# A paced weight stream under a scan, and an MLP whose weights are scaled a piece ahead, in a hybrid transformer block

## The chip, the cores and the metric

The kernel runs on one core of a Trainium2 chip. The metric is the time of one execution on the device in microseconds (us). Engines: PE (TensorE, matrix products), DVE (VectorE), ACT (ScalarE), POOL (GpSimd) and SP (issues transfers). TensorE's clock has two levels, 1.2 and 2.4 GHz; the profile gives the granted clock of a stretch as a share of the upper one.

## The reference, cut to what matters

```python
zl = modulate(rms_norm(xl, norm1_g), ml[0], ml[1]) @ w_in       # 2048 latent tokens, and 256 context tokens
yl_gla  = gla_mixer(...)     # gated linear attention, both directions
yl_rwkv = rwkv7_mixer(...)   # delta-rule state, both directions, 6 heads
yl_ret  = retention(...)     # 4 heads, both directions, then silu(g) * rms-normed output
xl = xl + ml[2] * (concat([yl_gla, yl_rwkv, yl_ret]) @ w_out)
hl = modulate(rms_norm(xl, norm2_g), ml[3], ml[4])
xl = xl + ml[5] * (square(relu(hl @ mlp_w1)) @ mlp_w2)          # 1024 -> 4096 -> 1024
return rms_norm(xl, final_norm_g)
```

Everything is float32; the width is 1024, chunks have 64 tokens.

## The kernel before

Tensors of weights and activations are split into a high and a low half (f16 pairs, or two fp32r parts), and a product is three matmuls. The work comes in stages, one after the other: the part of the input projection that the RWKV scan needs (to about 590 us), the scan stage (to about 2095 us), the output projection (to about 2320 us), the first half of the MLP (tokens 0 to 1023, to about 3085 us) and its second half.

**The scan stage** is written by a planner, `Order`. Its streams are generators; each writes some instructions and yields the planner time until it may go on, or a condition. `pick` takes, of the streams whose condition holds and which are ready, the one with the least position `pos()`; a stream's position runs evenly from `first` to `last` over its yields. All matmuls of the stage are recorded with one line, L1065; one goes by tiles. The streams are:

- the RWKV scan: `prepare` for each direction makes a block's factors, and the chains (`rw_chains`, L945) run 108 steps of 64 tokens one after the other, forward and backward together. A step has three products in PSUM (`ptf`, `ptb`): the state's, copied by ACT to `Ts`; the corrections', negated into `UV` half by DVE (L964) and half by ACT (L965); and the new state's, which DVE adds to the old into `SUV` (L975). `rw_finish` normalizes finished blocks of tokens.
- `ip_stream` (L450): the rest of the input projection, 86 tiles of 128 tokens in five groups of columns (`STREAM_T`), each 24 matmuls with tile `rh`, in pieces of six; its results go to memory (`zt`), where the mixers read them. In this text it is "the stream". `k.streamed` counts its finished groups. Its PSUM pool has one bank.
- the mixers: GLA heads, then the two retention pairs (`ret_pair`, L1655), which start when their group is finished; what `follow` adds (the row-wise finish, transposes `fpt`) runs beside them.

**The MLP** goes over 16 pieces fp of the hidden width, 256 columns each. `mlp_w1` (L1857) loads a piece's weights, takes the greatest magnitude (DVE reductions L1867, then `over_partitions`: a PE transpose L1850, a reduction L1852, a PE product with ones L1853), makes the scale, and from sums of the weight's blocks seven f16 weights `wo` (L1842, L1879, L1880). `hidden` makes seven products (L2041, bank `pu`) and from them the squared hidden values as `uh` and `ul` (L2068, L2070). Then eight blocks of 128 tokens t each take twelve products with w2 (L2105), added to `acc` by DVE (L2107): sixteen additions a piece. The second half reads the weights that the first has written (`w1d`, `w2d`).

The first piece's weight is made in `out_proj`, and the last norm there (`norms(7)`) and w2 come ahead of the first hidden products.

Code beside these stages is ordered by the tile framework's scheduler.

Of the kernel before, what the change touches and what calls it, by code (L numbers as in the profile page):

```python
# [22 lines left out]
P = 128  # L23
# [420 lines left out]
STREAM_T = [TV, TG[0:3], RET_T[0], RET_T[1], TG[3:5]]  # L444


def ip_stream(k, wp, ps):
# [10 lines left out]
    for g, cols in enumerate(STREAM_T):  # L458
# [485 lines left out]
def rw_chains(k, gs, nxt, j, blk, yT, done, bp, ps):  # L944
# [6 lines left out]
    for c in range(4):  # L951
        pt = [ps.tile([P, 3, 64], F32, tag="pc" + x, name="pt" + x, bufs=1) for x in "fb"]
# [87 lines left out]

class Order:

# [5 lines left out]
    def add(self, gen, first, last, count, lead=1e9):  # L1048
        s = Stream(gen, first, last, count, lead)
        s.ready = self.t  # L1050
        self.streams.append(s)
        return s
# [28 lines left out]
    def run(self):  # L1081
# [572 lines left out]
def ret_pair(k, p2, pool, ps):  # L1654
# [6 lines left out]
    nc.sync.dma_start(V.rearrange("p c h n -> p c (h n)"), grp(0, T, vc))  # L1661
# [4 lines left out]
    def keys(t0, n):  # L1666
        c0, nch = t0 // P, n // P
        if t0:
# [13 lines left out]
    yield 4  # L1682
    kd = keys(*TOKB[0])
    yield 4
    for bi, (t0, n) in enumerate(TOKB):
# [15 lines left out]
        if bi + 1 < len(TOKB):  # L1701
            kd = keys(*TOKB[bi + 1])
# [70 lines left out]
    k.fin = follow(k, 5, finish_rows(k, pool, ps, Y, ms, 2, 64, gc, k.col("rng", p2), 768 + 128 * p2))  # L1773


def follow(k, n, gen):
# [6 lines left out]
    return k.order.add(steps(), k.mix.pos() - 20, k.mix.pos() + 5, 10)  # L1783


def mixers(k, ps):
# [3 lines left out]
    with tc.tile_pool(name="mix", bufs=1) as mp:  # L1790
# [55 lines left out]
def over_partitions(k, ps, pool, x):  # L1846

    nc = k.nc
    pt = ps.tile([P, 512], F32, tag="p1", name="pmx")
    nc.tensor.transpose(pt[0:1, 0:P], x, k.ident)  # L1850
    m = pool.tile([1, 1], F32, tag="mx1", name="mx1")
    nc.vector.tensor_reduce(m, pt[0:1, 0:P], axis=AX.X, op=ALU.max)  # L1852
    nc.tensor.matmul(pt[:, P : P + 1], k.ones[0:1], m, start=True, stop=True)  # L1853
    return pt[:, P : P + 1]


def mlp_w1(k, fp, sp, tag, bufs, ws, wp, eng):  # L1857

# [404 lines left out]
```

## Time and profile before

| what | value |
|---|---|
| median of 3 runs | 3725.27 us (3703.3, 3725.27, 3731.29) |
| profiled execution | 3744.08 us, its span 3742.3 us |
| mean granted TensorE clock | 0.908 |
| PE busy | 3411.3 us, 91% |
| DVE, ACT, POOL busy | 2437.2, 1394.9, 685.7 us |

The views are read from the profiled execution, which took 0.5% longer than the median.

### The profile page before, as it was taken

The numbers are of one execution on the slowest core, as the hardware profiler recorded it, in microseconds if no ns is written. First come the engines' busy times: TensorE is split into PE (matmuls) and PEld (weight loads), VectorE is DVE, ScalarE is ACT, GpSimd is POOL, SyncE is SP. The second block draws the span as 40 slices with busy tenths as digits, with TensorE's granted clock in tenths as the row PEclk, the third lists the DMA queues.
The fourth block names the chain that finished last, engine by engine and source line by source line (L and its number), as shares of the span: only waits on it lengthen the run. The fifth ranks groups of instructions, "written<-read, shape, count | busy, mean of one in ns | idle before, by whom it ended". The sixth has DMA issues, their size and how long they took to land. (4 is left out here: it accounts for less than half of the span.)

```text
span 3742.3 us, 62893 instructions
## 1 busy us (share of the span) xinstructions
PE 3411.3 (91%) x23616; PEld 2272.0 (61%) x23616; DVE 2437.2 (65%) x5128; ACT 1394.9 (37%) x3097; POOL 685.7 (18%) x863
## 2 busy tenths in 40 slices
PE   6798999999998999989998598899999999999997
PEld 2444446676666766767776486555555556666665
DVE  7458785668856576674665488876777665444446
ACT  3355553344436255252434234333333342112113
POOL 3224443234413222222332100000000010000001
PEclk7898998988978799778888799999999999999998
DMA  7988876446634436333332387633333365223222
GB/s 228 202 229 252 249 214 198 133 135 191 163 115 126 104 105 153 76 102 104 96 98 84 136 201 258 218 130 123 125 124 124 111 184 186 89 89 119 89 89 97
DMA packets 534217, 547.09 MB, mean 146 GB/s; under 512 B 276475, under 2 KB 407366, under 8 KB 533134
## 3 DMA queue, kind: packets, MB, share of 16 engines
q1 hardware_dynamic: 533904, 542.99, 48.7%
q8 instruction: 188, 3.08, 0.4%
q14 instruction: 125, 1.02, 0.1%
HBM read 331.18 MB, written 187.55 MB: 139 GB/s over the span
## 5 line engine op out<-in xcount | busy, mean ns | idle before, releaser
L2041 PE MATMUL pu<-H,wo 128*128 128x512 f16 x2688 | 623.9, 386 | 23.9 <-ACT wo L1879 20.8
L2107 DVE TENSOR_TENSOR acc<-acc,pz 128x512 f32<-128x512 f32 x512 | 348.0, 686 | 376.2 <-PE pz L2105 372.8
L2041 PEld LDWEIGHTS <-wo 128*128 128x128 f16 x2688 | 254.2, 99 | 357.1 <-issue 58.4
L2105 PE MATMUL pz<-w2h,uh 128*128 128x512 f32 x1024 | 441.2, 431 | 26.0 <-ACT uh L2068 23.9
L2105 PE MATMUL pz<-w2l,uh 128*128 128x512 f32 x1024 | 411.4, 402 | 0.0
L2105 PE MATMUL pz<-w2h,ul 128*128 128x512 f32 x1024 | 396.8, 396 | 0.0
L1065 PE MATMUL pz<-rwh,rh 128*128 128x384 f16 (+1 forms) x1376 | 289.3, 342 | 8.5 <-DMA rh<-hd 5.9
L2120 POOL TENSOR_TENSOR acc<-acc,fg 128x1024 f32<-128x1024 f32 x10 | 24.0, 2416 | 1457.6 <-ACT acc L2119 1457.6
L1065 PEld LDWEIGHTS <-rh 128*128 128x128 f16 x2064 | 198.0, 105 | 134.6 <-issue 37.5
L2105 PEld LDWEIGHTS pz<-w2h,uh 128*128 128x128 f32 x1024 | 199.9, 195 | 83.6 <-ACT uh L2068 26.1
L2105 PEld LDWEIGHTS pz<-w2l,uh 128*128 128x128 f32 x1024 | 199.9, 195 | 41.4
L2105 PEld LDWEIGHTS pz<-w2h,ul 128*128 128x128 f32 x1024 | 195.8, 191 | 43.3
L2065 ACT ACTIVATE u<-u 128x512 f32<-128x512 f32 x64 | 36.8, 622 | 476.5 <-DVE s L2059 476.5
L425 PEld LDWEIGHTS <-wh 128*128 128x128 f16 (+2 forms) x1072 | 111.0, 107 | 151.1 <-issue 44.6
L425 PE MATMUL pz<-hT_hi,wh 128*128 128x512 f16 (+5 forms) x536 | 127.2, 379 | 42.0 <-ACT zs L428 23.8
L2053 ACT ACTIVATE s<-pu,iv 128x512 f32<-128x512 f32 x96 | 65.5, 686 | 259.3 <-PE pu L2041 258.0
L1065 PE MATMUL pz<-rwl,rh 128*128 128x384 f16 (+1 forms) x688 | 143.7, 339 | 0.0
L1065 PE MATMUL pg<-Z,BK 64*128 64x128 f32 (+1 forms) x864 | 138.4, 339 | 4.0 <-issue 1.9
L1988 PE MATMUL pz<-woh,yh 128*128 128x512 f32 x256 | 100.2, 406 | 28.2 <-DMA x<-in_w_out_dram 21.6
L1065 PEld LDWEIGHTS pg<-Z,BK 64*128 64x128 f32 x864 | 115.8, 233 | 16.8 <-issue 5.8
L425 PE MATMUL pz<-hT_hi,wl 128*128 128x512 f16 (+5 forms) x536 | 122.8, 366 | 0.0
L425 PE MATMUL pz<-hT_lo,wh 128*128 128x512 f16 (+5 forms) x536 | 121.0, 363 | 0.0
(526 smaller groups left out, 6915.8 us busy)
## 6 DMA issues: line engine op xcount, KB each, us to landing
rh<-hd SPq DMA_DIRECT2D x86, 512.0 KB
st<-in_mlp_w_dram SPq DMA_DIRECT2D x64, 512.0 KB
w1d<-wo SPq DMA_DIRECT2D x112, 256.0 KB
wo<-w1d SPq DMA_DIRECT2D x112, 256.0 KB
x<-in_x_dram SPq DMA_DIRECT2D x32, 512.0 KB
mw<-in_mod_w_dram SPq DMA_DIRECT2D x32, 512.0 KB
w2d<-w2h SPq DMA_DIRECT2D x32, 512.0 KB
w2d<-w2l SPq DMA_DIRECT2D x32, 512.0 KB
```

What stands on the lines that cost most here:

```text
L425: nc.tensor.matmul(pz[:M, o : o + step], a[:, kk, 0:M], b[:, kk, t0 + o : t0 + o + step], start=(i == 0), stop=(i == 23))
L1065: return op(out, lhs, rhs, **kw)
L1988: nc.tensor.matmul(pz, a[:, kk], w[:, kk, 512 * hf : 512 * hf + 512], start=(kk + i == 0), stop=(kk == KD - 1 and i == 2))
L2041: nc.tensor.matmul(bank, W[o][:, a, kk], H[o][:, 4 * b + kk], start=(i == 0), stop=(i == 11))
L2053: nc.scalar.activation(s, product(o), AF.Copy, scale=iv)
L2065: nc.scalar.activation(r, r, AF.Relu)
L2105: nc.tensor.matmul(pz, U[q][tb][u][:, ts], W2[q][w][:, cs], start=(i == 0), stop=(i == 5))
L2107: nc.vector.tensor_add(a[:, cs], a[:, cs], pz)
L2120: nc.gpsimd.tensor_mul(a, a, fg)
```

## The change

In the scan stage: `ip_stream` is paced. It gets a `period` in planner time, `PACE` (3.3) times the width of its piece over 384; `pick` takes it as soon as it is due and leaves it out before, except where nothing else is ready. Its PSUM pool has two banks. The last retention gates' group goes ahead of the second retention pair's columns. The chains' two directions share one PSUM tile, `pt`. `ret_pair` waits for tiles of the stream (`k.tile`) in place of whole groups and loads V block by block; the finish of pair 0 waits for four groups in place of five, and its position is later.

In the MLP: `mlp_w1` is split. `mlp_w1_load` loads the weight, sums its squares by ACT (L1880), and gets the scale from the sum's inverse root (`norm_scale`: one product with ones, L338, and five small DVE operations); it runs one piece earlier. `mlp_w1` is a generator that makes one of the seven weights behind each token block of the piece before. `over_partitions` is gone. `hidden` is the function `mlp_hidden`, and the first piece's call stands in `out_proj`, ahead of w2 and `norms(7)`.

```diff
-STREAM_T = [TV, TG[0:3], RET_T[0], RET_T[1], TG[3:5]]
+STREAM_T = [TV, TG[0:3], RET_T[0], TG[3:5], RET_T[1]]
...
+            k.stream.period = PACE * n / 384
...
+            k.tile = ti + 1
             yield 0
-        k.streamed += 1
+        k.streamed, k.tile = k.streamed + 1, 0
...
-        pt = [ps.tile([P, 3, 64], F32, tag="pc" + x, name="pt" + x, bufs=1) for x in "fb"]
+        pc = ps.tile([P, 2, 3, 64], F32, tag="pc", name="pt", bufs=1)
+        pt = [pc[:, d] for d in range(2)]
...
+        paced = [s for s in open_ if s.period and s.ready <= self.t]
+        for s in paced:
+            if s.due <= self.t or len(open_) == 1:
+                return s
+        if len(open_) > 1:
+            open_ = [s for s in open_ if not s.period] or open_
         head = min(s.pos() for s in open_)
         near = [s for s in open_ if s.pos() <= head + s.lead] or open_
         ready = [s for s in near if s.ready <= self.t]
         if ready:
             return min(ready, key=Stream.pos)
+        for s in paced:
+            if s.due <= self.t + 3 * s.period:
+                return s
...
+            if s.period:
+                s.due = max(s.due, self.t - s.period) + s.period
...
+    def there(i):
+        t0, n = TOKB[i]
+        return lambda: (k.streamed, k.tile) >= (2 + 2 * p2, (t0 + n) // P)
+
-    yield 4
+    yield there(0)
     kd = keys(*TOKB[0])
...
         if bi + 1 < len(TOKB):
+            yield there(bi + 1)
             kd = keys(*TOKB[bi + 1])
...
-    k.fin = follow(k, 5, finish_rows(k, pool, ps, Y, ms, 2, 64, gc, k.col("rng", p2), 768 + 128 * p2))
+    k.fin = follow(k, 4 + p2, finish_rows(k, pool, ps, Y, ms, 2, 64, gc, k.col("rng", p2), 768 + 128 * p2))
...
-    return k.order.add(steps(), k.mix.pos() - 20, k.mix.pos() + 5, 10)
+    return k.order.add(steps(), k.mix.pos() - 10, k.mix.pos() + 15, 10)
...
-                yield lambda: k.streamed >= 3 + p2
                 yield from ret_pair(k, p2, pool, ps)
...
-        nc.vector.tensor_reduce(am[:, h : h + 1], st[h], axis=AX.XY, op=ALU.max, apply_absolute_value=True)
-    nc.vector.tensor_max(am[:, :1], am[:, :1], am[:, 1:])
-    ar = sp.tile([P, 1], F32, tag="ar", name="ar")
-    nc.vector.tensor_scalar(ar, over_partitions(k, k.p1, sp, am[:, :1]), 1e-30, 2.0 ** -14, ALU.max, ALU.mult)
-    s = sp.tile([P, 1], F32, tag="s", name="s")
-    iv = k.iv[:, fp : fp + 1]
-    nc.vector.reciprocal(s, ar)
-    nc.vector.tensor_mul(iv, ar, k.h_inv2)
-    W = {}
+        sq = jp.tile([P, D], BF16, tag="sq", name="sq", bufs=1)
+        nc.scalar.activation(sq.rearrange("p (k n) -> p k n", k=4), st[h], AF.Square, accum_out=am[:, h : h + 1])
+    nc.vector.tensor_add(am[:, :1], am[:, :1], am[:, 1:])
+    s, ar = norm_scale(k, k.p1.tile([P, 512], F32, tag="p1", name="pnrm")[:, 0:1], k.w1s, am[:, :1])
+    nc.vector.tensor_mul(k.iv[:, fp : fp + 1], ar, k.h_inv2)
+    return st, s
...
+        yield o, w
...
+        U0 = mlp_hidden(k, H, up, W0, k.iv[:, 0:1])
         k.g2 = mod_row(k, w2, 3)
+        W2 = [mlp_w2(k, q, w2) for q in range(2)]
         norms(7, xs, ss[:, 14:16])
-        W2 = [mlp_w2(k, q, w2) for q in range(2)]
...
+        loaded = None if half else mlp_w1_load(k, 1, wp, "st", 2, wp)
...
-                W1 = mlp_w1(k, fp, (wp, wp0)[fp % 2], "st", 2, 1, k.w1, nc.vector)
                 W2 = [mlp_w2(k, 2 * fp + q, w2p) for q in range(2)]
-            U = hidden(*W1)
+            U = mlp_hidden(k, H, up, W1, k.iv[:, fp : fp + 1]) if fp or half else U0
+            following = iter(()) if half or fp == NF - 1 else mlp_w1(k, fp + 1, *loaded, (wp, wp0)[(fp + 1) % 2], 1, k.w1, nc.vector)
+            if not half and fp < NF - 2:
+                loaded = mlp_w1_load(k, fp + 2, (wp0, wp)[fp % 2], "st", 2, wp)
+            W1 = {}
...
+                W1.update([x for x in (next(following, None),) if x])
...
-            fps = es.enter_context(tc.tile_pool(name="iprps", bufs=1, space=PSUM, side="right"))
+            fps = es.enter_context(tc.tile_pool(name="iprps", bufs=2, space=PSUM, side="right"))
...
-            k.order.add(ip_stream(k, fp, fps), 0, 312, 345, 4)
+            k.stream = k.order.add(ip_stream(k, fp, fps), 0, 312, 345, period=PACE)
```

How the instructions stand then is read from the order of each engine's instructions. First PE at the stream's last product (`pz<-rwh,rh`) in the scan stage, before: `pm`, `pn`, `pk` are of `rw_finish`, `fpt` of the retention finish, `rpt` of the last retention pair.

```order
L1065 MATMUL pz<-rwh,rh 128x256
L1065 MATMUL py<-GB,UVb 64x64
L1065 MATMUL pm<-yT,bones 128x256
L1065 MATMUL pgt<-fsg,wg_1455 128x256
L1065 MATMUL pm<-yT,bones 128x256
L1065 MATMUL pgt<-fsg,wg_1455 128x256
L1065 MATMUL pn<-bones,sqf 128x2 x4
L1065 MATMUL pk<-ident,sqf 128x128 x2
L1065 MATMUL fpt<-ident,rY 128x128 x4
L1065 MATMUL rpt<-ident,rK 128x128 x4
L1065 MATMUL pk<-ident,sqf 128x128 x2
```

The same place, the stream's last product, after the change (`pt` is the chains' shared tile, `pg` a factor's product in `prepare`, `fpt<-ident,gY` the finish of a GLA head):

```order
L1073 MATMUL pz<-rwh,rh 128x384
L1073 MATMUL pt<-UVf,BKT 64x64 x2
L1073 MATMUL pt<-UVb,BKT 64x64 x2
L1073 MATMUL fpt<-ident,gY 96x128 x4
L1073 MATMUL py<-Z,SUVf 64x64 x2
L1073 MATMUL py<-Z,SUVb 64x64
L1073 MATMUL pk<-ident,sqf 128x128 x2
L1073 MATMUL pt<-SUVf,Z 64x64 x2
L1073 MATMUL pt<-SUVb,Z 64x64 x2
L1073 MATMUL py<-Z,SUVb 64x64
L1073 MATMUL pg<-Z,BK 128x128 x4
L1073 MATMUL pt<-Tsf,XT 64x64 x2
```

Before, the stream's last product stands behind the chains' last, among finish and retention; now chains, factors and finishes follow it.

PE in the first half of the MLP, around the product with ones that makes a scale, before (rows `pz` are the first products with w2 of the same piece):

```order
L2041 LDWEIGHTS wo
L2041 MATMUL pu<-H,wo 128x512
L1850 MATMUL pmx<-ident,am 1x128
L1853 MATMUL pmx<-mx_33529,ones 128x1
L2105 MATMUL pz<-w2h,uh 128x512
L2105 MATMUL pz<-w2l,uh 128x512
```

And around L338, in the same half, after:

```order
L1943 LDWEIGHTS wo
L1943 MATMUL pu<-H,wo 128x512
L338 MATMUL pnrm<-am,ones 128x1
L1943 LDWEIGHTS wo
L1943 MATMUL pu<-H,wo 128x512
L1943 LDWEIGHTS wo
```

The transpose and the product with ones stood between a piece's hidden products and its products with w2; now one product with ones stands among hidden products.

DVE in the first half of the MLP, from the last hidden products of a piece on, before (L1870 to L1874 make the scale, L1880 the low half of a weight, L1899 is w2's):

```order
L2049 SCALAR_TENSOR_TENSOR s_33260<-pu,iv_79,s_33260 128x512
L2049 SCALAR_TENSOR_TENSOR s_33259<-pu,iv_79,s_33259 128x512
L1852 TENSOR_REDUCE mx_33529<-pmx 1x1
L2070 TENSOR_TENSOR ul<-u_33304,uh 128x512
L1899 TENSOR_TENSOR st_33583<-st_33583,mrow 128x1024
L2070 TENSOR_TENSOR ul<-u_33305,uh 128x512
L1870 TENSOR_SCALAR ar<-pmx 128x1
L2070 TENSOR_TENSOR ul<-s_33260,uh 128x512
L1873 RECIPROCAL s<-ar 128x1
L1874 TENSOR_TENSOR iv_79<-ar,h_inv_3662 128x1
L2070 TENSOR_TENSOR ul<-s_33259,uh 128x512
L1880 SCALAR_TENSOR_TENSOR wo<-ws,s,wo 128x512
```

And where the scale is made after the change (L340 to L346 are `norm_scale`, L1895 is the low half of a weight, L1866 the sum of blocks, L1914 and L1918 are w2's, L1972 is `ul`):

```order
L1951 SCALAR_TENSOR_TENSOR s_34863<-pu,iv_79,s_34863 128x512
L1918 TENSOR_TENSOR w2l<-st_34845,w2h 128x1024
L340 TENSOR_SCALAR ar<-pnrm 128x1
L1918 TENSOR_TENSOR w2l<-st_34854,w2h 128x1024
L1895 SCALAR_TENSOR_TENSOR wo<-ws,sc,wo 128x512
L343 TENSOR_SCALAR sc<-ar 128x1
L1972 TENSOR_TENSOR ul<-s_34863,uh 128x512
L1866 TENSOR_TENSOR ws<-st_35330,st_35334 128x512
L344 TENSOR_SCALAR sc<-sc 128x1
L345 TENSOR_SCALAR sc<-sc 128x1
L346 RECIPROCAL ar<-sc 128x1
L1883 TENSOR_TENSOR iv_79<-ar,h_inv_3662 128x1
```

Before, the first weight follows the scale at once; now weights of the piece ahead stand among the operations of another piece's scale.

## Rows read from the trace of the kernel before

**Rows 1.** Windows by stage: window, length, busy us (count) by engine, PEclk, DMA.
```profile
600.00:2100.00 1500.00, 1374.97 (x14310) 1018.53 (x14309) 973.94 (x2612) 622.98 (x1748) 451.93 (x615) 0.85 0.42 119
2320.00:2400.00 80.00, 64.23 (x261) 40.04 (x260) 71.90 (x115) 31.95 (x50) 0.00 (x0) 0.89 0.85 284
2400.00:2900.00 500.00, 455.73 (x1933) 287.17 (x1932) 353.85 (x535) 157.55 (x247) 0.00 (x0) 0.93 0.37 127
3100.00:3600.00 500.00, 500.00 (x2246) 325.33 (x2245) 241.64 (x351) 105.59 (x189) 0.00 (x0) 1.00 0.31 104
```

**Rows 2.** Windows, scan, tile rh (stream) alone: PE, PEld, PEclk, DMA.
```profile
650.00:675.00 25.00, 11.94 (x66) 5.84 (x64) 1.00 0.50 151
...
725.00:750.00 25.00, 9.70 (x48) 4.03 (x48) 1.00 0.32 95
...
1250.00:1275.00 25.00, 2.95 (x9) 1.03 (x10) 0.50 0.44 107
1525.00:1550.00 25.00, 1.15 (x6) 0.39 (x4) 0.61 0.30 80
...
2025.00:2050.00 25.00, 0.00 (x0) 0.00 (x0) 0.71 0.30 93
2050.00:2075.00 25.00, 0.00 (x0) 0.00 (x0) 0.94 0.04 11
```

**Rows 3.** Windows of 200 us in the scan, columns as rows 1.
```profile
1000.00:1200.00 200.00, 181.83 (x1790) 124.44 (x1789) 118.42 (x333) 85.33 (x227) 54.34 (x100) 0.80 0.43 119
```

**Rows 4.** Waits of PE in the scan: total us, times, longest us.
```profile
PE fpt L1065 <- POOL rY L1463: 12.9, 4, 7.7
PE ptf L1065 <- ACT Tsf L958: 7.6, 7, 3.2
PE ptf L1065 <- DVE SUVf L975: 6.1, 9, 1.6
...
PE pz L1065 <- ACT rzs L480: 2.4, 4, 1.0
```

**Rows 5.** Accumulator additions, 2400:2900, then 3100:3600: busy us, mean ns, idle before.
```profile
L2107 DVE TENSOR_TENSOR acc<-acc,pz 128x512 f32<-128x512 f32 x172 | 115.9, 684 | 87.5 <-PE pz L2105 87.4
...
L2107 DVE TENSOR_TENSOR acc<-acc,pz 128x512 f32<-128x512 f32 x203 | 139.6, 687 | 208.9 <-PE pz L2105 208.0 <-issue 0.9
```

**Rows 6.** Waits of PE, first MLP half, 2400 to 3060 us.
```profile
PE pmx L1853 <- DVE mx L1852: 24.6, 13, 2.5
PE pu L2041 <- ACT wo L1879: 20.6, 6, 3.5
PE pz L2105 <- ACT uh L2068: 11.5, 7, 1.6
```

**Rows 7.** Timeline of PE, first MLP half: start us, us, instruction [idle before].
```profile
2526.56 0.38 PE L1853 MATMUL pmx<-mx,ones 1*128 1x1 f32 x2 [2.04 <-DVE mx L1852]
2528.58 0.80 PE L2105 MATMUL pz<-w2h,uh 128*128 128x512 f32 x1 [1.65 <-ACT uh L2068]
2529.18 0.63 PE L2105 MATMUL pz<-w2l,uh 128*128 128x512 f32 x1
...
2534.43 0.40 PE L2105 MATMUL pz<-w2l,uh 128*128 128x512 f32 x1
```

**Rows 8.** Waits of PE, 2320 to 2400 us.
```profile
PE pz L2105 <- ACT uh L2068: 9.2, 2, 8.4
PE pmx L1850 <- issue: 4.7, 1, 4.7
```

**Rows 9.** Groups: ACT Square at out_proj (2100:2400), DVE maximum (2400:3060).
```profile
L1995 ACT ACTIVATE sq<-x 128x1024 bf16<-128x1024 f32 x16 | 16.9, 1054 | 20.3 <-DVE x L1991 20.0
...
L1867 DVE TENSOR_REDUCE am<-st 128x1 f32<-128x1024 f32 x24 | 29.2, 1217 | 9.1 <-DMA st<-in_mlp_w_dram 8.6
```

**Rows 10.** Groups: ACT and DVE evictions of the chains, 600 to 2100 us.
```profile
L965 ACT ACTIVATE UVb<-ptb 64x64 f32<-64x64 f32 x108 | 23.5, 218 | 52.7 <-DVE UVb L964 52.1
...
L975 DVE SCALAR_TENSOR_TENSOR SUVb<-SUVb,Wd,ptb 64x64 f32<-64x64 f32 x210 | 58.6, 279 | 30.1 <-PE ptb L1065 22.6 <-ACT xo L844 3.5
```

More of the change, by code (lines that the diff above doesn't have):

```diff
@@ L1046, in __init__, with add @@
         self.nc, self.t, self.streams, self.mode = nc, 0.0, [], None
-    def add(self, gen, first, last, count, lead=1e9):
+    def add(self, gen, first, last, count, lead=1e9, period=None):
         s = Stream(gen, first, last, count, lead)
-        s.ready = self.t
+        s.ready = s.due = self.t
+        s.period = period
         self.streams.append(s)
@@ L1843, in summed, with mlp_w1_load @@
     return out
[L1846 to L1857, printed above, removed]
+def mlp_w1_load(k, fp, sp, tag, bufs, jp):
     nc = k.nc
@@ L1915, in mlp_w2_kept, with mlp_hidden, product, new @@
     return vh, vl
+def mlp_hidden(k, H, up, W, iv):
+    nc = k.nc
+    def product(o):
+        bank = k.p1.tile([P, 512], F32, tag="p1", name="pu")
+        i = 0
+        for a, b in ((0, 0), (1, 0), (0, 1)):
+            for kk in range(4):
+                nc.tensor.matmul(bank, W[o][:, a, kk], H[o][:, 4 * b + kk], start=(i == 0), stop=(i == 11))
+                i += 1
+        return bank
+    def new(nm):
+        return up.tile([P, 512], F32, tag=nm, name=nm, bufs=1)
+    def add(out, o, s):
+        nc.vector.scalar_tensor_tensor(out, product(o), iv, s, ALU.mult, ALU.add)
+    s1, s2, s3 = (new(nm) for nm in ("s1", "s2", "s3"))
+    for o, s in ((1, s2), (2, s3), (0, s1)):
+        nc.scalar.activation(s, product(o), AF.Copy, scale=iv)
+    u10, u01 = new("u10"), new("u01")
+    add(u10, 3, s2)
+    add(u01, 4, s3)
+    nc.vector.tensor_sub(s3, s3, s2)
+    nc.vector.tensor_add(s1, s1, s3)
+    nc.vector.tensor_sub(s2, u10, u01)
+    nc.vector.tensor_add(s2, s2, s1)
+    add(s2, 6, s2)
+    add(s1, 5, s1)
+    U = [[], []]
+    for q, r in ((1, u10), (0, u01), (0, s2), (1, s1)):
+        nc.scalar.activation(r, r, AF.Relu)
+        nc.scalar.activation(r, r, AF.Square)
+        uh = up.tile([P, 512], F32R, tag="uh", name="uh")
+        nc.scalar.copy(uh, r)
+        ul = up.tile([P, 512], F32R, tag="ul", name="ul")
+        nc.vector.tensor_tensor(ul, r, uh.bitcast(F32), ALU.subtract)
+        U[q].append((uh, ul))
+    return [U[0][::-1], U[1]]
 def out_proj(k, es, H, hp):
@@ L2031, in mlp @@
     ps = es.enter_context(tc.tile_pool(name="mlps", bufs=4, space=PSUM))
-    def hidden(W, iv):
-        def product(o):
-            bank = k.p1.tile([P, 512], F32, tag="p1", name="pu")
-            i = 0
-            for a, b in ((0, 0), (1, 0), (0, 1)):
-                for kk in range(4):
-                    nc.tensor.matmul(bank, W[o][:, a, kk], H[o][:, 4 * b + kk], start=(i == 0), stop=(i == 11))
-                    i += 1
-            return bank
-        def new(nm):
-            return up.tile([P, 512], F32, tag=nm, name=nm, bufs=1)
-        def add(out, o, s):
-            nc.vector.scalar_tensor_tensor(out, product(o), iv, s, ALU.mult, ALU.add)
-        s1, s2, s3 = (new(nm) for nm in ("s1", "s2", "s3"))
-        for o, s in ((1, s2), (2, s3), (0, s1)):
-            nc.scalar.activation(s, product(o), AF.Copy, scale=iv)
-        u10, u01 = new("u10"), new("u01")
-        add(u10, 3, s2)
-        add(u01, 4, s3)
-        nc.vector.tensor_sub(s3, s3, s2)
-        nc.vector.tensor_add(s1, s1, s3)
-        nc.vector.tensor_sub(s2, u10, u01)
-        nc.vector.tensor_add(s2, s2, s1)
-        add(s2, 6, s2)
-        add(s1, 5, s1)
-        U = [[], []]
-        for q, r in ((1, u10), (0, u01), (0, s2), (1, s1)):
-            nc.scalar.activation(r, r, AF.Relu)
-            nc.scalar.activation(r, r, AF.Square)
-            uh = up.tile([P, 512], F32R, tag="uh", name="uh")
-            nc.scalar.copy(uh, r)
-            ul = up.tile([P, 512], F32R, tag="ul", name="ul")
-            nc.vector.tensor_tensor(ul, r, uh.bitcast(F32), ALU.subtract)
-            U[q].append((uh, ul))
-        return [U[0][::-1], U[1]]
     NF, ENDS = DFF // 256, (1, 3, 5, 7)
@@ L2223, in tile_hybrid_block @@
             fp = es.enter_context(tc.tile_pool(name="ipr", bufs=1, side="right"))
-            fps = es.enter_context(tc.tile_pool(name="iprps", bufs=1, space=PSUM, side="right"))
-            k.order, k.inputs, k.streamed, k.fin = Order(nc), 0, 0, None
+            fps = es.enter_context(tc.tile_pool(name="iprps", bufs=2, space=PSUM, side="right"))
+            k.order, k.inputs, k.streamed, k.tile, k.fin = Order(nc), 0, 0, 0, None
             rw_scan(k, bp, ps)
```

19 lines of the change are left out of this document (11 added, 8 removed).

## The prediction

> **What bounds the kernel now.** I read the windows by stage first. TensorE is busy nearly everywhere, so the question in each stage is whether it is idle, or busy at half clock. In the scan stage (600 to 2100 us) it is busy 1374.97 of 1500 us, but at a mean granted clock of 0.85; in the first half of the MLP it is busy 455.73 of 500 us at 0.93; in the second half 500 of 500 us at 1.00 [rows 1]. The second half is thus at TensorE's floor, the first half is short of it, and VectorE (353.85 of 500 us) bounds neither. A mean clock of 0.85 between the levels 2.4 and 1.2 GHz means 30% of the stage at the lower one.
>
> The second view is the stage's windows with the stream's tile (rh) alone: how many of its matmuls fell into 25 us, and which clock was granted. With 66 or 48 of them the clock is 1.00; with 9, 6 and none it reads 0.50, 0.61 and 0.71, once 0.94 without any [rows 2]. That TensorE is busy does not protect the clock: from 1000 to 1200 us it is busy 181.83 of 200 us at 0.80 [rows 3]. The third view, the waits of TensorE in the scan, shows no single large stall: the longest group is the transposes of the last retention finish (12.9 us in 4 waits), and each of the chains' waits sums to 6 to 8 us in a whole stage [rows 4].
>
> For the MLP I counted accumulator additions (16 for each of the 16 pieces fp of the hidden layer): 172 in 500 us of the first half, 203 in 500 us of the second [rows 5], so 46.5 us and 39.4 us a piece. The waits name the cause: 24.6 us on the maximum over partitions, 20.6 us on the scaled weights, 11.5 us on the hidden values, 56.7 us in 660 us [rows 6]. The timeline shows what they cost beyond themselves: after 2.04 and 1.65 us of idleness the second product's matmuls take 0.63 us each, where they take 0.40 us six microseconds later [rows 7]: the clock fell to its lower level behind the stall.
>
> **MLP, first half.** The weight's scale is taken away from the place where it is waited for. Before, TensorE transposes the maxima, VectorE reduces them (L1852), TensorE spreads the result, VectorE makes the scale and the first weight, and only then can the next hidden products start. After, one matmul with ones (L338) gives the scale a whole piece earlier, and each of the seven weights is made behind one of the eight token blocks of the piece before. In the changed order the PE row behind L338 is more of the same hidden products, and nothing there returns to PE. The two stalls and the half-clock stretch behind them should go. The whole gap to the second half is 46.5 − 39.4 = 7.1 us a piece, over 15 pieces 107 us: the upper bound. I take 5.5 of the 7.1, **−82 us**, because something stays late: all seven weights, both w2 pieces and the additions share VectorE with the first half's 353.85 us per 500, and the next piece's weights now stand in VectorE's row between the additions that TensorE's banks wait for. The lower bound is 40 us: if the waits on the scaled weights and the hidden values (20.6 and 11.5) stay with their clock loss and only the maximum's go, 24.6/56.7 of 107 is 46.
>
> What it adds: two Squares a piece on ScalarE, 1054 ns each [rows 9], so 2.1 us in about 41 us, on an engine busy 157.55 of 500 us [rows 1]; idle time hides it. It takes two reductions of 1217 ns a piece off VectorE [rows 9] and adds some six operations of one column. Were ScalarE's cover gone (the Square queued before a cast of hidden values, waiting for its DMA), each piece would pay up to 2.1 us: 32 us of the 82.
>
> **MLP, start.** The first hidden products are put ahead of the last norm and of w2. Before, PE waits there 9.2 us for hidden values, whose arithmetic stands in VectorE's row among that norm's, and 4.7 us before a transpose of maxima that is gone after [rows 8]. The stretch from 2320 to 2400 us has 64.23 us of PE in 80. I take **−10 us** of those 13.9; ends −15 and +5, the latter if the norm, now behind, delays block t = 7's products.
>
> **Scan.** Work is not removed; the stream is put elsewhere. In the order before, the stage has 8,645 rows of matmuls and the stream's last stands behind the chains' last product; after, it ends 78% of the way, and 1,926 rows follow without it, which carry the last 29 to 30 of the 108 chain steps, retention pair 1 and its finish. Ahead of that the stream comes evenly: gaps of over 100 other matmuls fall from 10 to 4. The sum in microseconds at full clock: the stage is 1500 × 0.85 = 1275 of them. The stream's 2,064 matmuls, at 11.94/66 = 0.18 us [rows 2], are 374, the rest 901. The 1,926 rows are 29% of the 6,581 that are no stream, 264; the part ahead of them is 1275 − 264 = 1011. Then the clocks. The part with the stream would have 2,064 matmuls in about 1,070 us, 48 in 25 us, where the row reads 1.00; the mean of windows mixes dense and thin, so I take 0.95: 1064 us. For the part without, the four rows of [rows 2] with under ten average 0.69, the last two, which are of retention work without chains, 0.83; I take 0.72: 367 us. Together 1431, **−69 us**; I round to −65, for the shared bank below. Ends: 0.90 and 0.69 give 1123 + 383, +6; 1.00 and 0.83 give 1011 + 318, −171. For the range I take +10 and −140, since in both ends the two clocks err together.
>
> The other edits of the stage are small. The retention pairs no longer wait for whole groups, and pair 0's finish no longer waits for the stream's end: the end of the stage before is retention and finish alone after the chains, with PE waiting 12.9 us for the finish [rows 4]; after, the chains are last, and their last few steps, with a finish of theirs behind, wait for themselves. I set one against the other, 0 within ±15. The stream's second bank removes at most the wait on its eviction, 2.4 us [rows 4].
>
> **The shared bank.** Both directions' chain products go into one bank. In the order with its waits, the backward negation on VectorE now waits for ScalarE's forward one, as both read one tile; before, the two had banks of their own: at most one ScalarE eviction of 218 ns [rows 10] and a like one of VectorE more in each of 108 steps, 47 us were nothing else waiting; and nothing, if the in-order PE gets to the next chain matmul later than that, which the small chain waits of [rows 4] suggest (6.1 us over 108 steps). Below zero: one wait of PE in place of two can save no more than such a group of waits, 6 us. I take 4. The Trainium skill speaks against this edit: "PSUM — Partial Sum Buffer", section "Summary: rules for kernel authors", says that PSUM being read while matmuls run should lie in a different bank from theirs. By that rule the steps would pay the bound, 47 us, and the forecast would be some 40 us later; no run here shows it yet.
>
> **Sum.** −65 − 82 − 10 = −157 on the profiled 3744.08 us, which is 0.5% above the median of the runs shown, 3725.27. 3587 × 0.995 gives **3569 us**.
>
> **The rivals.**
> *The clock eats the scan's gain.* The last fifth of the scan falls to the lower level: at 0.50, as in the thinnest row [rows 2], it takes 528 us, and with 0.95 before it the stage is 92 us slower; at 0.60 it takes 440, the stage 1504, no gain. For it: the rows with few stream matmuls. Against it: 0.94 in the last of them, and that retention and finish fill this part. At 0.60 the time is 3744 − 92 = 3652, or **3634**. Chance 0.14.
> *The clock holds wherever PE is busy.* Then the streamless part runs at 0.94 too: 281 + 1064, −155, and the MLP −92: 3497, or **3480**. Against it speak [rows 3]. Chance 0.06. The Trainium skill, "TensorE: Matmul & The Clock Gate", section "HAM oscillation", has idle gaps as what lowers the clock. The trace agrees in the MLP [rows 7], hardly in the scan [rows 3].
> *The MLP keeps its period.* Each piece's Square or weight waits behind something slower (DMA of the weight, VectorE's row), and only 20 us go: 3744 − 65 − 20 − 5 = 3654, or **3636**. For it: VectorE is the second busiest there. Against it: at 41 us a piece it would be about 75% busy. Chance 0.07.
> *The shared bank makes the chains the bound; slower.* Each step's evictions queue, three on the path: 0.22 for the copies and 0.44 for the negations at 218 ns each, 0.56 for two more state updates of 279 ns [rows 10], 1.2 us, and the idle PE loses clock behind each, 2 us in all. Over 108 steps 216: 3744 − 157 + 216 = 3803, or **3784**. It decides from 157/108 = 1.45 us a step. Against it: evictions mostly lie under other matmuls. Chance 0.03.
> *Both halves give nothing*, **3725**: 0.05.
>
> **How the numbers follow.** The forecast has the remaining 0.65. Its own bounds are −140 − 107 − 15 = −262 (3465) and +10 − 40 + 5 = −25 (3700); both ends together are unlikely. The range 3460 to 3685 holds the forecast nearly whole, the first three rivals, and leaves out about 0.12. A measurement of this kernel can tell about 1% from no change, since three runs spread over 3703 to 3731. Faster by over 1% (under 3688): the forecast and the first three rivals, less a little of their upper edges, 0.89. Within 1%: 0.07. Slower: 0.04.
>
> **What would show it.** Right: the first MLP half at 41 to 42 us a piece, clock near 1.00, no wait on a maximum; scan windows at 0.95 until the stream ends, near 0.7 after, the stage some 65 us shorter; the chains' waits as small as in [rows 4]. Wrong: waits of PE on `wo` or `uh` of over 2 us a piece; a streamless part of over 440 us; waits of `pt` on the chains' evictions that sum to tens of microseconds. What would upset the forecast most is the clock of the scan's last fifth, as two levels a factor of two apart lie over 264 us of work.

## The result, and the profile after

The changed kernel takes 3674.36 us (median of 10 runs, 3655.15 to 3694.35) against 3726.09 us (10 runs, 3697.58 to 3745.76): a ratio of 0.987, 95% interval 0.983 to 0.991. The forecast was 3569 us, a gain three times as large. The profiled execution took 3669.31 us, its span is 3667.5 us, at a mean clock of 0.903; before it were 3744.08, 3742.3 and 0.908. So the two profiled executions differ by 75 us, more than the medians' 52.

First the windows by stage of the changed kernel, with the columns of [rows 1]:

```profile
600.00:2100.00 1500.00, 1366.87 (x14269) 1041.78 (x14267) 961.96 (x2564) 616.40 (x1740) 451.31 (x612) 0.82 0.42 118
2320.00:2400.00 80.00, 58.45 (x241) 38.58 (x240) 62.70 (x111) 36.18 (x57) 0.00 (x0) 0.85 0.77 258
2400.00:2900.00 500.00, 491.72 (x2217) 316.21 (x2216) 384.33 (x631) 215.75 (x353) 0.00 (x0) 0.99 0.42 150
3100.00:3600.00 500.00, 500.00 (x2247) 323.25 (x2246) 240.24 (x348) 108.19 (x193) 0.00 (x0) 1.00 0.29 96
```

The MLP did what was forecast: its first half is at PE 491.72 of 500 us and a clock of 0.99, where [rows 1] have 455.73 and 0.93. The scan did the opposite: its clock fell from 0.85 to 0.82. The same view, cut where the stream's last matmul ends (1705 us) and where the stage ends (2113 us):

```profile
578.00:1705.00 1127.00, 1026.84 (x10803) 750.24 (x10802) 746.27 (x1886) 494.70 (x1373) 371.64 (x525) 0.89 0.49 138
1705.00:2113.00 408.00, 370.85 (x3615) 307.97 (x3613) 228.47 (x730) 132.51 (x391) 84.27 (x93) 0.63 0.21 61
```

Up to the stream's end the clock is 0.89, behind it 0.63, for 408 us. The stage takes 1535 us in all in this profile; before it took 1510. The kernel before, cut in the same way at 2021 and 2091 us:

```profile
581.00:2021.00 1440.00, 1344.91 (x14112) 988.12 (x14110) 949.89 (x2539) 605.39 (x1714) 435.28 (x600) 0.86 0.44 122
2021.00:2091.00 70.00, 48.91 (x306) 39.94 (x303) 26.15 (x75) 22.23 (x44) 18.64 (x18) 0.78 0.17 53
```

The windows of the stream's tile, answering to [rows 2], show the edge:

```profile
1600.00:1625.00 25.00, 9.05 (x49) 4.38 (x49) 1.00 0.38 114
1625.00:1650.00 25.00, 2.77 (x8) 1.21 (x8) 0.82 0.10 30
1650.00:1675.00 25.00, 1.82 (x5) 0.68 (x5) 0.84 0.28 78
...
1700.00:1725.00 25.00, 5.20 (x30) 2.65 (x28) 0.75 0.63 180
1725.00:1750.00 25.00, 0.00 (x0) 0.00 (x0) 0.50 0.29 79
1800.00:1825.00 25.00, 0.00 (x0) 0.00 (x0) 0.52 0.08 24
```

With 49 stream matmuls the clock is at its upper level, and in these windows without any it reads 0.50 and 0.52; with 8 and 5 it still reads 0.82 and 0.84. TensorE is as busy behind the edge (370.85 of 408 us) as ahead of it (1026.84 of 1127). The windows of all engines show 50 us behind the edge in which it hardly waits at all, at a clock of 0.51:

```profile
1800.00:1850.00 50.00, 49.96 (x339) 43.35 (x340) 16.77 (x44) 13.15 (x40) 7.09 (x9) 0.51 0.12 33
```

So its waits behind the edge, answering to [rows 4], are not the reason for that clock; the longest groups are

```profile
PE py L1073 <- DVE UVf L967: 14.1, 4, 8.0
PE pt L1073 <- DVE SUVb L978: 5.5, 4, 2.9
PE pk L1073 <- ACT sqf L782: 3.8, 4, 1.8
```

In the MLP the additions to `acc` from 2460 to 2960 us, answering to [rows 5]:

```profile
L2130 DVE TENSOR_TENSOR acc<-acc,pz 128x512 f32<-128x512 f32 x196 | 132.1, 684 | 73.1 <-PE pz L2128 72.5
```

and the only wait of PE from 2400 to 3060 us, answering to [rows 6]:

```profile
PE pnrm L338 <- DVE am L1881: 8.3, 1, 8.3
```

196 additions in 500 us are 40.8 us a piece. Such a count is rough, since a window cuts pieces off and long and short pieces alternate (43 and 37 us). From the start of a piece's first addition to that of the next, the third to the fifteenth piece take 39.8 us on average in the changed kernel and 47.6 before; in the second half they take 39.9 and 40.0. The 56.7 us of waits of [rows 6] have become 8.3. But those belong to something new. From 2260 to 2480 us, at the MLP's start, PE waits twice, 13.0 us and those 8.3, for the sum that the scale's product (L338) needs:

```profile
PE pnrm L338 <- DVE am L1881: 21.2, 2, 13.0
PE pz L2128 <- ACT uh L1970: 8.2, 1, 8.2
```

The queue of transfers (SPq) shows that two loads of a weight (`st`, L1878) are issued there behind seven stores of the norm (`h`), which hold it for 15 us:

```profile
2354.78 15.30 SPq L2021 DMA_DIRECT2D h<-hl  x7
...
2372.41 0.98 SPq L1878 DMA_DIRECT2D st<-in_mlp_w_dram  x2
```

### The profile page after: what moved, and what is told of

Its sections match the earlier page's. It is cut to its first block, busy times and chain, and to the rows that moved or that the text cites. A ratio compares the mean times of both kernels' runs of the same rounds, so it can differ in the third digit from the quotient of the medians.

```text
span 3667.5 us, 62713 instructions
## 1 busy us (share of the span) xinstructions
PE 3369.1 (92%) x23600; PEld 2283.4 (62%) x23600; DVE 2390.8 (65%) x5128; ACT 1425.5 (39%) x3161; POOL 686.6 (19%) x863
## 3 DMA queue, kind: packets, MB, share of 16 engines
q1 hardware_dynamic: 534032, 542.99, 49.8%
## 5 line engine op out<-in xcount | busy, mean ns | idle before, releaser
L1943 PE MATMUL pu<-H,wo 128*128 128x512 f16 x2688 | 608.5, 380 | 0.0
L2128 PE MATMUL pz<-w2h,uh 128*128 128x512 f32 x1024 | 424.4, 418 | 11.9 <-ACT uh L1970 11.4
L2128 PE MATMUL pz<-w2l,uh 128*128 128x512 f32 x1024 | 402.6, 393 | 0.0
L1073 PE MATMUL pz<-rwh,rh 128*128 128x384 f16 (+1 forms) x1376 | 274.4, 333 | 14.5 <-DMA rh<-hd 14.5
L2128 PEld LDWEIGHTS pz<-w2l,uh 128*128 128x128 f32 x1024 | 193.7, 189 | 39.9
L1073 PE MATMUL pg<-Z,BK 64*128 64x128 f32 (+1 forms) x864 | 149.5, 350 | 10.8 <-DMA Z<-AR 6.0
L1073 PEld LDWEIGHTS pg<-Z,BK 64*128 64x128 f32 x864 | 127.7, 245 | 24.9 <-issue 5.9
```

Of the source, the lines that this page charges most:

```text
L1073: return op(out, lhs, rhs, **kw)
L1943: nc.tensor.matmul(bank, W[o][:, a, kk], H[o][:, 4 * b + kk], start=(i == 0), stop=(i == 11))
L2128: nc.tensor.matmul(pz, U[q][tb][u][:, ts], W2[q][w][:, cs], start=(i == 0), stop=(i == 5))
```

## The experiments

All times are medians; the ratio is to the kernel before on the same chip. A row of windows is given as above, up to the stream's end and behind it.

| run | what | us | ratio (95%) |
|---|---|---|---|
| e1 | MLP's part alone | 3636.61 | 0.976 (0.971 to 0.980) |
| e2 | scan's part alone | 3762.53 | 1.011 (1.007 to 1.015) |
| e3 | chains' banks apart, one stream bank | 3643.19 | 0.981 (0.974 to 0.988) |
| e4 | one stream bank | 3624.88 | 0.975 (0.970 to 0.981) |
| e5 | matmuls added behind the stream | 3651.33 | 0.982 (0.978 to 0.985) |
| e6 | one load buffer for the stream | 3676.85 | 0.986 (0.983 to 0.988) |
| e7 | MLP's part and the banks, old plan | 3712.23 | 0.996 (0.993 to 0.999) |
| e8 | the same with one stream bank | 3636.26 | 0.978 (0.972 to 0.984) |
| e9 | pace 4.2 | 3650.35 | 0.982 (0.975 to 0.989) |
| e10 | pace 4.2, one stream bank | 3631.48 | 0.974 (0.966 to 0.982) |
| e11 | one load buffer, one stream bank | 3675.88 | 0.986 (0.979 to 0.994) |
| e12 | e4 with the matmuls of e5 | 3601.10 | 0.967 (0.961 to 0.974) |
| e13 | second piece's weight loaded earlier | 3640.74 | 0.981 (0.973 to 0.989) |
| e14 | e12 with the load of e13 | 3601.94 | 0.968 (0.961 to 0.975) |
| e15 | e14 with twice the added matmuls | 3626.64 | 0.974 (0.967 to 0.982) |

**e1 and e2: the halves apart.** e1 takes the hunks of the diff from `over_partitions` to `mlp`, e2 the others, such as

```diff
e1
-                W1 = mlp_w1(k, fp, (wp, wp0)[fp % 2], "st", 2, 1, k.w1, nc.vector)
+            following = iter(()) if half or fp == NF - 1 else mlp_w1(k, fp + 1, *loaded, (wp, wp0)[(fp + 1) % 2], 1, k.w1, nc.vector)
e2
-            k.order.add(ip_stream(k, fp, fps), 0, 312, 345, 4)
+            k.stream = k.order.add(ip_stream(k, fp, fps), 0, 312, 345, period=PACE)
```

> Kernel before with the MLP's part of the change alone (weight's scale a piece ahead, weights behind the token blocks, first hidden products ahead of the last norm). Theory A (the scan's part loses what it should gain, the MLP's part gains what was forecast): 3726 - 93 = about 3633 us, faster than the whole change; first half 40 to 41 us a piece. Rival B (the gain of the whole change is spread, the MLP's alone is smaller): 3660 or more.

> Kernel before with the scan's part alone (order of groups, pace, shared chain bank, two stream banks, retention's waits). Theory A: the stream's last product comes some 300 to 400 us before the stage ends, the rest runs near 0.7 of the clock, the time is 3726 + 20 (3735 to 3755). Rival B: 3700 or less.

The MLP's part alone gains 89 us (forecast: 92), the scan's alone loses 36. Theory A holds, with a scan 8 us worse than its bounds. The two add up: −89 + 36 = −53, measured −52. The scan of e2 is the changed kernel's, its matmuls in the same order but for some 15 of 14,415. Behind the stream its profile reads

```profile
1724.00:2108.00 384.00, 344.95 (x3606) 285.64 (x3602) 228.81 (x730) 132.11 (x391) 84.86 (x93) 0.69 0.22 65
```

against 408 us at 0.63 above. Two profiles of that stretch can thus differ by some 25 us and 0.06 of the clock with no edit in it.

**e3 and e4: which banks.**

```diff
e3
-        pc = ps.tile([P, 2, 3, 64], F32, tag="pc", name="pt", bufs=1)
-        pt = [pc[:, d] for d in range(2)]
+        pt = [ps.tile([P, 3, 64], F32, tag="pc" + x, name="pt" + x, bufs=1) for x in "fb"]
e3 and e4
-            fps = es.enter_context(tc.tile_pool(name="iprps", bufs=2, space=PSUM, side="right"))
+            fps = es.enter_context(tc.tile_pool(name="iprps", bufs=1, space=PSUM, side="right"))
```

> The changed kernel with its paced plan, but a PSUM bank for each direction of the chains again and one bank for the stream. In the built order the stream then ends at 95% of the stage's matmuls instead of 78%, and the chains at 98% instead of 99.6%. Theory A1 (the bank arrangement lets the framework's scheduler run the stream ahead of the plan, and what follows without it runs at half clock): the stage is 50 to 90 us shorter, 3585 to 3625 us, clock over 0.85 up to the stream's end. Rival A2 (the shared bank's waits cost directly, the order does not matter): 108 steps times at most 0.43 us, 3630 to 3674 with the clock in the last quarter still near 0.7. Rival A3 (retention and finish behind the chains again cost what is gained): about 3670.

> The changed kernel with one stream bank, the chains' shared bank kept. In the built order the stream ends at 81% instead of 78%. Theory A1: nearly no change, within 15 us of 3674. If the second stream bank by itself gained anything: slower by over 15 us. If A2: no change either, since the shared bank stays.

A1 missed in both. The windows of e3:

```profile
579.00:1964.00 1385.00, 1287.45 (x13616) 946.93 (x13613) 905.03 (x2376) 578.42 (x1650) 424.50 (x593) 0.86 0.45 125
1964.00:2083.00 119.00, 96.73 (x800) 77.11 (x799) 70.04 (x240) 45.23 (x110) 27.14 (x26) 0.68 0.19 60
```

The windows of e4:

```profile
581.00:1729.00 1148.00, 1048.45 (x11285) 763.48 (x11285) 772.77 (x1981) 513.05 (x1430) 374.72 (x541) 0.90 0.50 140
1729.00:2052.00 323.00, 298.45 (x3129) 245.82 (x3128) 196.24 (x635) 112.22 (x333) 69.76 (x78) 0.72 0.20 60
```

In e3 the stream runs to 1964 us, as A1 wanted, and the clock ahead of that is 0.86, as in the kernel before, not 0.9 or more: the stage takes 1504 us. In e4, which was to change nothing, the stage takes 1471. So an early end of the stream is not by itself what costs. A2's time fits e3, but not e4, which keeps the shared bank and is by the medians the faster of the two, in overlapping intervals: no cost of the shared bank shows. That the second stream bank costs some 50 us was new: the four runs of e4 (3614 to 3646) all lie below the ten of the changed kernel (3655 to 3694).

**e5: is it the clock?** Added, in the chains' steps of the last seven blocks:

```diff
+        def fill(x):
+            if j == 2 and blk >= 2:
+                pf = ps.tile([P, 2, 64], F32, tag="pb", name="pf")
+                for _ in range(FILL):       # 10
+                    nc.tensor.matmul(pf, k.ident.bitcast(BF16)[:, 1::2], x.bitcast(BF16)[:, :, 1::2], start=True, stop=True)
...
+        fill(gs[0].SUV[:, :, c, :])
...
+        fill(gs[0].UV[:, :, c, :])
```

> The changed kernel with work added: in the last 28 chain steps, which follow the stream, 20 bf16 matmuls of 128 columns a step (560 in all), which multiply the chains' own tiles by the identity into a bank that nothing reads. At 0.06 to 0.1 us each they are 34 to 56 us of added work at full clock. Theory A (the stretch behind the stream, 407 us, is long because PE gets the lower clock there): the clock there rises from 0.63 to 0.8 or more, and the stage gets no longer or shorter in spite of the work, -70 to +5 us: 3605 to 3680. Rival A2 (the stretch is long by the chains' waits and by its work): +35 to +90 us, 3710 or more, the clock in the stretch unchanged.

The windows of e5:

```profile
579.00:1697.00 1118.00, 1019.48 (x10810) 747.35 (x10808) 743.70 (x1886) 494.68 (x1372) 372.75 (x525) 0.89 0.50 139
1697.00:2079.00 382.00, 333.49 (x4169) 278.85 (x4170) 233.68 (x730) 131.69 (x390) 84.46 (x92) 0.82 0.23 65
```

The stretch behind the stream has 4169 matmuls instead of 3615 and takes 382 us instead of 408, its clock rises from 0.63 to 0.82, and the kernel is 23 us faster by the medians (the intervals of the two ratios overlap a little). The rival wanted 35 us or more on top. Two things limit this. The same stretch without added matmuls took 384 us at 0.69 and 0.68 in the profiles of e2 and e13, so that the higher clock is beyond the scatter, and a shorter stretch is not: what is shown is that 554 more matmuls cost it no time. And they moved the others: ahead of the edge 10,780 of 10,805 matmuls stand in the changed kernel's order, behind it 1,729 of 3,610, so that the new order may have a part in the rise.

That the lower clock lengthens the stretch shows in one product of the retention, of the same shape in both kernels: at a clock of 0.94 (before, 2050 to 2075 us) it takes 281 ns, at 0.51 (changed, 1800 to 1850 us) 422 ns.

```profile
L1065 PE MATMUL rpy<-rV,rA 128*128 128x64 f32 x46 | 9.2, 281 | 0.4
...
L1073 PE MATMUL rpy<-rV,rA 128*128 128x64 f32 x31 | 10.0, 422 | 0.0
```

**e6 and e11: hold the stream back.** With one load buffer the stream stands nearly at the stage's end in the built order.

```diff
-            h = wp.tile([P, 2, KD, P], F16, tag="rh", name="rh", bufs=2)
+            h = wp.tile([P, 2, KD, P], F16, tag="rh", name="rh", bufs=1)
```

> The changed kernel, shared chain bank and two stream banks kept, with one buffer for the stream's loaded tiles (rh) instead of two. In the built order the stream then ends at 96% of the stage instead of 78%, spread evenly. Theory A1 (what costs is that the stream ends early): the stage is 40 to 80 us shorter, 3595 to 3635. Rival A4 (a matmul of the stream buys its clock wherever it stands; spreading it thins the clock of the rest): the clock is near 0.86 over the whole stage, as in the kernel before, and the stage within 20 us of 1510, 3640 to 3670. Rival A5 (the load waits): PE waits of over 40 us for rh, 3700 or more.

> One load buffer and one stream bank. With one load buffer the stream ends at 96% of the order with either count of banks, so the second bank can't run it ahead. Theory A6 (the bank costs through the order alone): within 15 us of the 3677 of the run with one load buffer and two banks. Rival A7 (two banks cost by themselves on the chip, whatever the order): 40 to 60 us faster, about 3625.

The windows of e6:

```profile
579.00:2018.00 1439.00, 1302.11 (x13773) 960.68 (x13772) 909.54 (x2394) 584.29 (x1661) 423.97 (x593) 0.85 0.44 121
2018.00:2130.00 112.00, 91.84 (x641) 73.36 (x641) 66.65 (x224) 42.74 (x100) 26.06 (x26) 0.66 0.19 58
```

Its longest group of waits of PE in the stage:

```profile
PE pz L1073 <- DMA rh<-hd: 34.6, 23, 4.6
```

A1 falls: the stream spans the stage and the stage takes 1551 us (its profiled run is the slowest of five). A4 is right on the clock (0.85, the kernel before had 0.86) but not on the time, which lies between its bounds and A5's: 34.6 us of waits for loads (5.9 in the kernel before) are rival A5's mechanism at nearly its size. In e11 the second bank makes no difference (3676 and 3677), as A6 has it. So the bank costs nothing where another buffer holds the stream, which speaks for a cost through the order.

**e7 and e8: the banks under the plan of before.** The MLP's part, the shared chain bank, and two stream banks or one; no pace, the old order of groups.

```diff
e7 and e8, against e1
-        pt = [ps.tile([P, 3, 64], F32, tag="pc" + x, name="pt" + x, bufs=1) for x in "fb"]
+        pc = ps.tile([P, 2, 3, 64], F32, tag="pc", name="pt", bufs=1)
+        pt = [pc[:, d] for d in range(2)]
e7
-            fps = es.enter_context(tc.tile_pool(name="iprps", bufs=1, space=PSUM, side="right"))
+            fps = es.enter_context(tc.tile_pool(name="iprps", bufs=2, space=PSUM, side="right"))
```

> The MLP's part, and of the scan's part only the banks: shared chain bank and two stream banks under the plan of before (no pace, old order of groups, old waits of the retention). Stream's end in the built order: 77%. Theory A1: the banks alone make the scan's loss, 3665 to 3685, near the whole change's 3674. If the pace makes it: near 3637, as the MLP's part alone.

> As the last, but with one stream bank: shared chain bank under the plan of before, and the MLP's part. Stream's end in the built order: 90%. Theory A1 as amended by the run with one stream bank (the second stream bank costs some 50 us, the shared chain bank nothing): 3625 to 3645. If the shared bank costs by itself: 3660 or more.

The windows of e7:

```profile
579.00:1726.00 1147.00, 1058.74 (x10730) 763.72 (x10729) 729.41 (x1855) 492.02 (x1363) 354.35 (x513) 0.86 0.48 135
1726.00:2158.00 432.00, 385.13 (x3689) 318.24 (x3687) 239.89 (x757) 136.01 (x397) 95.91 (x104) 0.63 0.20 58
```

The windows of e8:

```profile
579.00:1889.00 1310.00, 1201.28 (x12796) 884.92 (x12794) 871.57 (x2206) 560.77 (x1583) 411.48 (x577) 0.88 0.46 130
1889.00:2071.00 182.00, 154.53 (x1623) 125.28 (x1624) 112.09 (x407) 65.60 (x177) 40.06 (x41) 0.74 0.18 54
```

The second stream bank costs 76 us here, even more than expected: behind the stream 432 us at 0.63, against 182 at 0.74. The shared chain bank costs nothing that these runs can tell (3636, e1 3637, either to within some 25 us). Under two banks the plan of the change (pace, order of groups and waits of the retention together) is 38 us better than that of before.

**e9 and e10: another pace,** with two banks and with one (e10 has e4's edit too).

```diff
-PACE = 3.3
+PACE = 4.2
```

> The changed kernel with its pace slowed from 3.3 to 4.2, two stream banks. In the built order the stream ends at 74% (78% with 3.3). If the plan's pace sets the stream's place on the chip: later end, 3600 to 3640. Theory A6 (with two banks the framework's scheduler runs the stream ahead whatever the plan says, and the stretch without it has the lower clock): 3665 to 3700, stream's end near 1700 us, the clock behind it under 0.7.

> The same with one stream bank; the stream ends at 81% of the built order. Theory A6: 30 us or more faster than the same pace with two banks, 3620 to 3645. If the gain of one bank at pace 3.3 was an accident of that order: within 15 us of the two-bank run.

The windows of e9:

```profile
580.00:1592.00 1012.00, 930.23 (x10223) 671.81 (x10222) 694.00 (x1741) 476.97 (x1320) 346.33 (x501) 0.94 0.54 150
1592.00:2087.00 495.00, 444.01 (x4196) 368.97 (x4194) 277.01 (x875) 151.01 (x446) 109.60 (x118) 0.63 0.20 58
```

The slower pace moved the stream's end earlier, to 1592 us, where a plan that sets its place would have moved it later. A6 has the clock behind it right (0.63) and missed the rest: the end lies 108 us ahead of the 1700 it named, and the time 15 us below its bound, with 0.94 in the part ahead. The gap between two banks and one is 19 us with overlapping intervals, where A6 wanted 30 or more, and in the profiles the two stages take 1507 and 1508 us: at this pace a cost of the bank is not settled.

**e12: one stream bank and the added matmuls,** the edits of e4 and e5 together.

> One stream bank with the 560 added matmuls behind the stream. Theory A (the clock behind the stream still costs there, 180 of 323 us at half clock): 3590 to 3620, faster than the 3625 without them. Rival: what was to gain is gone with one bank, and the added work shows: 3630 to 3670.

The windows of e12:

```profile
580.00:1732.00 1152.00, 1054.05 (x11288) 769.46 (x11286) 773.85 (x1981) 514.02 (x1430) 378.31 (x541) 0.89 0.50 140
1732.00:2046.00 314.00, 287.24 (x3686) 244.57 (x3686) 199.64 (x635) 112.01 (x332) 70.00 (x78) 0.85 0.21 62
```

Theory A holds: the stage takes 1466 us, and the kernel is 24 us faster than e4, 73 faster than the change; its slowest run (3604.69) is faster than e4's fastest (3614.06). Here too the added matmuls moved the others behind the edge and hardly any ahead of it. Its four runs lie within 7 us (3597.59 to 3604.69), where the ten of the changed kernel spread over 39.

**e13, e14 and e15: the stall at the MLP's start, and more added work.**

```diff
-        loaded = None if half else mlp_w1_load(k, 1, wp, "st", 2, wp)
+        loaded = None if half else mlp_w1_load(k, 1, wp0, "st", 2, wp0)
...
-                loaded = mlp_w1_load(k, fp + 2, (wp0, wp)[fp % 2], "st", 2, wp)
+                loaded = mlp_w1_load(k, fp + 2, (wp, wp0)[fp % 2], "st", 2, wp0)
e15, also
-FILL = 10
+FILL = 20
```

> The changed kernel, but the second MLP piece's weight (and with it every even one's place) is loaded into the pool that exists before the last norm, so that its load no longer waits for that norm's stores. Theory (the 13 and 8 us that PE waits for the first two scales are this load): the wait on L338 falls from 29 us to under 8, the pieces one and two together take some 15 to 21 us less, 3653 to 3660 us. Rival (the stall is the transfers' total load there, 258 GB/s, or ScalarE's row): the wait stays, or moves to another operand, and the time is within 6 us of 3674.

> The same on top of one stream bank and the 560 added matmuls behind the stream: 3580 to 3590 if both effects add up, against 3601 without the moved load.

> As the last, with twice the added matmuls (1120). They are 30 to 50 us more of PE work at full clock. With 560 the clock behind the stream is 0.85, so at most 15% of 314 us, 47 us, is left to gain: within -15 to +25 us of the last run, more likely slower.

PE's waits of e13 from 2260 to 2480 us:

```profile
PE pz L2128 <- DVE acc L2130: 13.0, 1, 13.0
PE pnrm L338 <- DVE am L1881: 9.7, 1, 9.7
```

The wait for the scale fell from 21.2 us (the 29 of the expectation counted the second wait twice) to 9.7, and 13.0 us for `acc` came in its place, which is also loaded there: the rival's "moves to another operand". The median of e13 is 34 us below the change's, in overlapping intervals and outside what either theory expected, but that need not be the load: the scan's matmuls stand in the same order in both (but for some 15), and the profiled stage took 1508 us in place of 1535, nearly all of it behind the stream:

```profile
1700.00:2084.00 384.00, 347.94 (x3613) 288.43 (x3611) 229.13 (x730) 132.75 (x391) 84.69 (x93) 0.68 0.22 65
```

e14, whose runs scatter less, shows the load's worth: nothing (3602, e12 3601), where 11 to 21 us were expected. e15's clock behind the stream rises to 0.92,

```profile
1735.00:2071.00 336.00, 306.66 (x4250) 264.92 (x4248) 198.16 (x635) 112.41 (x333) 70.83 (x78) 0.92 0.20 58
```

and the kernel is 25 us slower than e14, at the edge of what was expected: from 560 matmuls to 1120 the added work costs more than the clock gives.

## Why the prediction was wrong

**MLP, right in sum, with its terms off.** Forecast were −82 and −10, together −92; e1 has −89 for the two. By the starts of the additions a steady piece went from 47.6 to 39.8 us, as short as in the second half, so that the whole gap came back and not 5.5 of 7.1 us, and nothing "stays late" on VectorE. Against that stands the start: the waits of [rows 8] were to shrink by 10 us, and PE waits 21.2 us for two scales, and 8.2 us for hidden values are still there; the first piece takes 72.2 us to the next one's first addition, where it took 49.8. The two errors cancel, so that the sum came out is in part luck. I had moved the hidden products past the last norm, but not asked what a norm that ends later holds up: the second piece's weight goes into a pool that takes over the norm's memory, and its load stands behind the norm's stores. ScalarE's Squares are hidden in the steady pieces, as argued.

**Scan, the step that failed: "I take 0.95 ... I take 0.72".** Where 65 us were to be gained, e2 loses 36. The work was sized right. At the measured clocks the parts are 1127 × 0.89 = 1003 and 408 × 0.63 = 257 us at full clock; forecast were 1011 and 264. The clocks were wrong, both on the same side: 0.89 and 0.63 make 1535 us of the 1431 forecast. The same order of matmuls read 0.87 and 0.69 in e2, 0.89 and 0.68 in e13, with stages of 1529 and 1508 us: the part with the stream missed its 0.95 in all three.

The trace of the kernel before held better values. [rows 2] are picked windows; others with as many stream matmuls read lower, such as

```profile
675.00:700.00 25.00, 8.46 (x44) 4.16 (x45) 0.80 0.48 156
...
1150.00:1175.00 25.00, 11.35 (x47) 4.84 (x46) 0.73 0.50 125
```

Of all 59 windows of 25 us from 600 to 2075 us, the 15 with 40 to 49 stream matmuls average 0.90, and the 10 with under ten 0.68. The part with the stream has 46 in 25 us. With these two the forecast's own work makes 1011 / 0.90 + 264 / 0.68 = 1512 us, a scan that gains nothing: the end of the bounds that the prediction put at +6.

Under the sizes lies the step from a denser stream to a gain. Clock times time is the work, waits included, and over the stage it hardly differs: 1293 us at full clock in the kernel before (1440 × 0.86 + 70 × 0.78), 1260 in the changed one, 1272 in e3, 1266 in e4, 1297 in e6, 1259 in e7, 1263 in e9. So the stage's time goes by its mean clock, and that lies between 0.80 (e7) and 0.86 (the kernel before, e4) in all of them, wherever the stream stands; only kernels with matmuls added have more, e5 0.87 and e12 0.88. What packing the stream gains in one part is lost in the other: e9 has 0.94 ahead, 0.63 behind and 0.84 over the stage. Within these clocks the stage takes 1471 to 1579 us, of which 27 us is what the same order differs by (the change and e13). Even without the second stream bank the scan's part is worth little: e4 is 12 us faster than e1, in overlapping intervals, where 65 were forecast.

**What set the order.** I read it from the built program and saw the stream end at 78%, but priced only what that meant, and not which edit made it. Both banks' edits do. Counted in the traces, 98% of the stage's matmuls stand ahead of the stream's end in the kernel before, 89% with the chains' shared bank (e8), 74% with the second stream bank as well (e7); under the new plan 94% without either (e3), 78% with the shared bank (e4), 75% with both (the change). Only the second stream bank costs, 49 us in the one plan (e4) and 76 in the other (e7 and e8), and I had costed it at a gain of at most 2.4 us. As e4 ends the stream nearly as early as the change, the place of the end is not what costs; what in the order of two banks lowers the mean clock, the runs don't show. The row of [rows 4] showed what the bank's absence cost, and could not show what its presence would move.

**The rivals.** *The clock eats the scan's gain* had the right mechanism for the part without the stream and 0.14; it kept 0.95 ahead of it and put the stage's change at 0, it was +25, and its time is 40 us short. The shared bank was not the slower rival, and its 4 us are too small for these runs: e8 and e1 are equal. The Trainium skill, "PSUM — Partial Sum Buffer", section "Summary: rules for kernel authors", asks for another bank where PSUM is read while matmuls run; a cost near the 47 us that the prediction worked out as its bound doesn't show here. *The clock holds wherever PE is busy* is refuted: 49.96 of 50 us busy at 0.51. The idle gaps that the Trainium skill names ("TensorE: Matmul & The Clock Gate", "HAM oscillation") are not what lowers it there; with matmuls added it is higher, in e5, e12 and e15.

What stays open: which of the matmuls behind the stream go with the lower clock, and how much of the rise in e5 and e12 is the added matmuls' and how much the new order's. Why e4's stretch behind the stream is at 0.72 and the changed kernel's at 0.63 to 0.69, with the same kinds of work in it, is open too. At pace 4.2 the banks' difference is within the intervals.

## What to carry to other kernels

Where many small matmuls hold a stage, the granted clock is part of its cost: size a reordering by the mean clock over whole stretches, and expect that moving the large matmuls moves the clock with them. Average over all windows of a kind, not over those that come to hand. A buffer that seems only to remove a wait can also change the order that the scheduler builds; read from the built order which edit moved what, and undo the edits one at a time. When a stage's last step is put later, look at who takes over its memory.

## What was not expected of the hardware

Added matmuls that nothing reads made the kernel faster: with 560 of 128 columns behind the stream the clock there is 0.85 in place of 0.72 and the kernel 24 us faster (e12 against e4); with 1120 it is 0.92, and the time is back (e15). In e12 the order of the other matmuls behind the stream changed too. The four runs spread over 32 us in e4, 7 in e12 and 5 in e14; but over 28 in e5 and 23 in e15, so that the added matmuls alone don't steady them. The same scan order took 1535 us in one profile and 1508 in another (the change and e13), and 24 of these 27 us lie behind the stream, at the low clock.

TensorE without a gap did not hold its upper clock: 49.96 of 50 us busy with small fp32 products, at 0.51.
